# Second products of the FFNs: the residual is loaded into the sum tiles before the first product, and every product is added to it

## The chip, the cores and the metric

The kernel runs on one core of one Trainium2 chip. The metric is the device time of one execution in microseconds (us). The median of 3 runs before the change is 2866.83 us (2863.23 to 2869.62).

## What is computed

One layer of a hybrid decoder over 1024 prompt tokens and 64 sample tokens, width 1024, all in float32: a half-step SwiGLU FFN, a token mixer (a pooling branch and a state-space branch), and a second half-step FFN, each behind an RMSNorm and added to its input, then a final RMSNorm. The change touches only how the two FFNs end:

```python
def swiglu(x, w_in, w_out):
    gu = x @ w_in
    g, u = gu[..., :D_FF], gu[..., D_FF:]
    return (jax.nn.silu(g) * u) @ w_out
...
        x = x + 0.5 * swiglu(rmsnorm(x, norm_ffn1[l]), ffn1_w_in[l], ffn1_w_out[l])
...
        x = x + 0.5 * swiglu(rmsnorm(x, norm_ffn2[l]), ffn2_w_in[l], ffn2_w_out[l])
```

D_MODEL is 1024 and D_FF is 2816. The plain x of the sum is the residual.

## The kernel before

Data lies with channels on the 128 partitions and tokens along the row. The 1088 tokens are two "halves": h=0 with 512 columns, h=1 with 576 (`NTOK`). A [128 x 512] or [128 x 576] tile of x belongs to a channel block m (0 to 7) and a half. Every float32 operand of a matmul is split into a high part (`wh`, `hh`) made by ScalarE (ACT) and a low part (`wl`, `hr`/`hp`) made by VectorE (DVE), and three matmuls (high x high, high x low, low x high) stand for one.

**The second matrix of an FFN** (`second`, lines 772 to 874) is multiplied by a Strassen-like scheme of seven products, in the order `ORDER2 = "4251736"`. For product p the weights are one block of `w_out` or the sum or difference of two (`BLOCKS2`; the addition is on POOL, L760), and the other operand is one of seven combinations of the hidden activations, which lie in HBM as `xq[p]` since the FFN's first half. Each product runs over 11 pieces `kk` of the hidden width, in two blocks, m0=0 and m0=2. A block has 132 matmuls and ends with four PSUM banks. So each FFN has 14 such blocks; the two stretches are called here the first and the second stage.

**Evictions.** At the end of a block, `add` (L815) puts each bank into the sum tiles `C[m, h]`, 16 tiles of the pool "fx" (17 buffers). `INTO2` says where product p goes and with which sign. The first contribution to a place is a copy with scale 0.5 on ACT (L828); later ones are `scalar_tensor_tensor` on DVE (L830): sum = 0.5 * product + sum. By `INTO2`, product 4 is wholly first contributions (12 copies in each of its two blocks), and products 2 and 5 each have 4 first and 6 later ones in a block: 40 copies in a stage. Evictions are traced at the priority `HP_EV` = 60.

**The residual** (L800). x lies in HBM as `xspill[h][m]`. During products 5, 1, 7 and 3 (`RES2`) four of its tiles each are loaded into `xr` tiles of the pool "act" (42 buffers) by SP's DMA queue (L805) and added to the sums on DVE (L812).

**What sets the order.** The code is written in the order of the matmuls; `pe[0]` counts estimated TensorE time. A `Chain` is a generator with a due time: after each `kk` piece `tick()` steps the chains that are due, and what a step issues is traced at that place. `fetch_x` (L777) is such a chain: it loads the 11 pieces of the next product's operand (`t`, L791: `hr<-xq`, or `hp<-xq` for products 4, 5 and 7, whose first eight pieces lie in the pool "pair" with 8 buffers) and splits them on ACT (L781) and DVE (L782) some loads later. Weights come by L754 (`wraw`, 6 buffers), are split by L768 on ACT and L769 on DVE (`wh`, `wl`, 3 buffers each), at the priority `HP` = 40. The framework orders the instructions of each engine by priority and readiness when the program is built, and each engine then takes its own in that order. All DMAs named here are issued from SP. The sums of hidden activations that make the last piece of `xq` are still done on POOL (L677 to L698) while product 4 begins; its place in the code is after the second run of weights (`run[0] == 2`, L859).

`after(0, ...)` is called once product 7 is done and begins the next norm for h=0; `half` and `after(1, ...)` take h=1 after products 3 and 6.

Of the kernel before, what the change touches and what calls it, by code (L numbers as in the profile page):

```python
# [11 lines left out]
AF = mybir.ActivationFunctionType  # L12
ALU = mybir.AluOpType

P = 128
# [14 lines left out]
HALVES = (0, 1)  # L30
NTOK = (512, 576)
# [30 lines left out]
ORDER2 = "4251736"  # L62
# [3 lines left out]
INTO2 = {"1": ((0, 0, 1), (1, 1, 1)), "2": ((1, 0, 1), (1, 1, -1)), "3": ((0, 1, 1), (1, 1, 1)),  # L66
         "4": ((0, 0, 1), (1, 0, 1)), "5": ((0, 0, -1), (0, 1, 1)), "6": ((1, 1, 1),), "7": ((0, 0, 1),)}
IN_PAIRS = "457"
RES2 = {2: (0, (4, 5, 6, 7)), 3: (0, (0, 1, 2, 3)), 4: (1, (0, 1, 2, 3)), 5: (1, (4, 5, 6, 7))}
X_AT, X_PACE, X_LAG, X_LAG_END = 2.0, 1.6, 6, 4  # L70
RES_PACE = 3.0
SUM_PACE = 1.5


# [1 line left out]
def tile_hybrid_pool_ssd_macaron(  # L76
# [10 lines left out]
    V, S, T, G = nc.vector, nc.scalar, nc.tensor, nc.gpsimd  # L87
    dma = nc.sync.dma_start
# [7 lines left out]
    def nm(s):  # L96
        uid[0] += 1
        return f"{s}_{uid[0]}"

    def act(shape=(P, 576), dt=F32, name="a"):  # L100
        return sp.tile(list(shape), dt, tag="act", bufs=N_ACT, name=nm(name))

    def pair(n, name="hl"):
        t = sp.tile([P, 2, 576], F32R, tag="pair", bufs=N_PAIR, name=nm(name))
        return t[:, 0, :n], t[:, 1, :n], t
# [16 lines left out]
    def fx(dt=F32, name="x"):  # L122
        if stage["name"] == "mix":
            return act((P, 576), dt, name)
        return stage["p"].tile([P, 592], dt, tag="fx", bufs=N_FX, name=nm(name))

    def psum(tag="ps", name="ps"):
        npd = stage["npd"]
        return stage["ps"].tile([P, 512], F32, tag=tag, bufs=npd if tag == "pd" else 8 - npd, name=nm(name))
# [18 lines left out]
    def start(gen, delay=0.0):  # L148
        c = Chain(gen, delay)
        chains.append(c)  # L150
        return c
# [13 lines left out]
    def finish(c):  # L165
        while not c.done:
            c.step()

    def tick():
        while chains:  # L170
            c = min(chains, key=lambda q: q.due)
            if c.due > pe[0]:
                return
            c.step()

    def mm(out, lhsT, rhs, start=True, stop=True, free=False):
        T.matmul(out, lhsT, rhs, start=start, stop=stop, skip_group_check=free)  # L177
        pe[0] += max(out.free_size(), 64) / 2400.0 * (1 if rhs.dtype == F32R else 4)
# [85 lines left out]
    xspill = [[dp.tile([P, NTOK[h]], F32, tag=f"xs{h}_{m}", name=f"xspill{h}_{m}") for m in range(KD)] for h in HALVES]  # L264
# [506 lines left out]

    def second(wo, after, half):

        X, C, touched = {p: [] for p in ORDER2}, {}, set()
        n = 2 * NQ

        def fetch_x(p, kks, pace, lag=X_LAG):  # L777
            loaded = []

            def part_x(t, a):  # L780
                S.activation(a[:, :n], t[:, :n], AF.Identity)  # L781
                V.tensor_tensor(t[:, :n].bitcast(F32R), t[:, :n], a[:, :n].bitcast(F32), op=ALU.subtract)  # L782
                X[p].append((a, t.bitcast(F32R)))

            for kk in kks:
                if p in IN_PAIRS and kk < N_PAIR:
                    a, t, _ = pair(576, "hp")
                    t = t.bitcast(F32)
                else:
                    t, a = act((P, 576), F32, "hr"), act((P, 576), F32R, "hh")  # L790
                dma(t[:, :n], xq[p][kk])  # L791
                loaded.append((t, a))
                if len(loaded) > lag:
                    part_x(*loaded.pop(0))
                yield pace
            while loaded:
                part_x(*loaded.pop(0))
                yield pace

        def residual(h, ms):  # L800
            loaded = []
            for m in ms + (None,):
                if m is not None:
                    t = act((P, NTOK[h]), name="xr")
                    dma(t, xspill[h][m])  # L805
                    loaded.append((m, t))
                    yield RES_PACE
                    if len(loaded) < 2:
                        continue
                m_, t = loaded.pop(0)  # L810
                o = C[m_, h][:, : NTOK[h]]
                V.tensor_tensor(o, o, t, op=ALU.add)  # L812
                yield RES_PACE

        def add(pt, m, side, c, sign):  # L815
            if side:
                to = [(1, NA + NQ * c, 0, NQ)]
            else:
                to = [(0, 0, 0, NQ)] if c == 0 else [(0, NQ, 0, NQ - NA), (1, 0, NQ - NA, NA)]
            new = (m, side) not in touched  # L820
            if c:
                touched.add((m, side))
            for h, at, of, w in to:
                if (m, h) not in C:
                    C[m, h] = fx(name="x")
                o = C[m, h][:, at : at + w]
                if new:
                    S.activation(o, pt[:, of : of + w], AF.Copy, scale=0.5 * sign)  # L828
                    continue
                V.scalar_tensor_tensor(o, pt[:, of : of + w], 0.5 * sign, o, op0=ALU.mult, op1=ALU.add)  # L830

        finish(start(fetch_x(ORDER2[0], range(NKK - 1), 0.0)))
        ahead = []
        for at, p in enumerate(ORDER2):
            if at + 1 < len(ORDER2):
                last = at + 2 == len(ORDER2)
                ahead.append(start(fetch_x(ORDER2[at + 1], range(NKK), *((1.4, X_LAG_END) if last else (X_PACE, X_LAG))),
                                   15.0 if last else X_AT if at else 6.0))
            if at in RES2:
                res = start(residual(*RES2[at]), 3.0)  # L840
            for m0 in (0, 2):
                pts = [[psum("ps" if j and m0 and at < 5 else "pd", "po") for _ in range(2)] for j in range(2)]
                kps = [(kp,) for kp in range(0, NKK, 2)]
                if at >= 5:
                    kps = [kps[0] + kps[1]] + kps[2:-2] + [kps[-2] + kps[-1]]
                for run in kps:
                    W2 = [(kp, min(2, NKK - kp), second_weights(wo, p, kp, min(2, NKK - kp), m0)) for kp in run]
                    for j in range(2):
                        for kp, n2, W in W2:
                            for k in range(n2):  # L850
                                while len(X[p]) <= kp + k:
                                    ahead[at - 1].step()
                                xh, xl = X[p][kp + k]
                                for i, (w, x) in enumerate(((0, xh), (0, xl), (1, xh))):
                                    for c in range(2):
                                        mm(pts[j][c][:, :NQ], W[w][:, k, j * P : (j + 1) * P], x[:, c * NQ : (c + 1) * NQ],
                                           start=kp + k == 0 and i == 0, stop=kp + k == NKK - 1 and i == 2)
                                tick()
                    if at == 0 and m0 == 0 and run[0] == 2:  # L859
                        while summing:  # L860
                            finish(summing.pop())
                        finish(start(fetch_x(p, range(NKK - 1, NKK), 0.0)))
                with tc.high_priority(HP_EV):
                    for j in range(2):
                        for c in range(2):
                            for y, side, sign in INTO2[p]:
                                add(pts[j][c], 4 * y + m0 + j, side, c, sign)
            if at in RES2:
                finish(res)
            if p == "7":  # L870
                after(0, [C[m, 0] for m in range(KD)])
            if p == "3" and half:
                half(1, [C[m, 1] for m in range(KD)])
        after(1, [C[m, 1] for m in range(KD)])
# [967 lines left out]
    for h in HALVES:  # L1842
# [9 lines left out]
        if h == 1:  # L1852
            o = []
            prep2.append((start(norm_parts(reload(0), 0, i_g2, o, 2.0)), o))
            c = prep2[0][0]
# [135 lines left out]
```

## Time and profile before

| | us |
|---|---|
| median of 3 runs | 2866.83 |
| lowest, highest run | 2863.23, 2869.62 |
| profiled execution, its time | 2863.49 |
| span of the profiled execution (first to last instruction) | 2861.7 |
| TensorE matmuls busy | 2766.0 (97% of the span) |
| VectorE busy | 1867.4 (65%) |
| ScalarE busy | 1362.0 (48%) |
| GpSimd busy | 1367.7 (48%) |
| first stage, first to last block of L856's matmuls | 528.8 to 779.1 |
| second stage | 2598.4 to 2846.2 |

The span lies 1.8 us below the profiled execution's own time. Matmul rows are pipelined and overlap, so a busy TensorE is read from its waits and from the length of a block. In the views "PE" is TensorE, "po" a block's PSUM bank, and an idle time is put down to what ended it ("<-").

### The profile page before, as it was taken

To read this page: it belongs to the slowest core of one execution; us is meant where nothing else is said; L and a number is where in the kernel's file an instruction comes from. 1 tells how busy PE (TensorE), PEld (TensorE's weight loads), DVE (VectorE), ACT (ScalarE), POOL (GpSimd) and SP (SyncE) were. 2 spreads that over 40 slices of the span, in tenths; PEclk is the share of its full clock that TensorE was granted. 3 is DMA by queue.
4 is the path that set the end of the run, shared out by engine and by line. 5 is a ranking of instruction groups with operands and counts; after the bars stand their busy time and mean duration, and the time that the engine had idled before them with its cause. 6 is when DMAs were issued, how large, how long until landed. Compare 5 with 4: busy or idle time off the path is not lost.

```text
span 2861.7 us, 54691 instructions
## 1 busy us (share of the span) xinstructions
PE 2766.0 (97%) x19834; PEld 2595.6 (91%) x19834; DVE 1867.4 (65%) x2904; ACT 1362.0 (48%) x3024; POOL 1367.7 (48%) x1406
## 2 busy tenths in 40 slices
PE   7999999999999999999999999999999999999998
PEld 5999999899889999999997887678999999998997
DVE  6665655777884485867675767766665544457775
ACT  5444444643454555554545545566233434435433
POOL 6566576443442365554632334233225766664432
PEclk9999999999999999999999999999999999999999
DMA  4565554798745455554368679887775323337965
GB/s 134 174 212 189 180 166 143 245 299 254 242 130 162 146 174 166 183 159 138 96 218 251 203 247 283 259 270 226 232 252 172 115 95 95 99 111 258 292 207 183
DMA packets 533488, 548.02 MB, mean 192 GB/s; under 512 B 42836, under 2 KB 373704, under 8 KB 533208
## 3 DMA queue, kind: packets, MB, share of 16 engines
q1 hardware_dynamic: 533200, 544.51, 59.8%
q8 instruction: 156, 2.56, 0.4%
q14 instruction: 116, 0.95, 0.1%
q10 hardware_dynamic: 16, 0.00, 0.0%
HBM read 391.82 MB, written 152.78 MB: 190 GB/s over the span
## 4 chain that ended last, share of the span: by engine, by line
PE 74%; DMA 9%; DVE 6%; issue 4%; POOL 3%; ACT 3%; SPq 1%; POOLq 0%; ACTq 0%; DVEq 0%
PE pw L177 45%; PE po L177 8%; PE pso L177 4%; PE pg L177 3%; PE pbp L177 3%; PE pwo L177 3%; PE pu L177 2%; DMA hr<-xq 2%; DMA hp<-xq 1%; DMA ea<-eacd 1%; DMA wraw<-in_ffn_w_out_dram 1%; PE pgm L177 1%; DMA ab<-acsd 1%; DVE hr L782 1%; PE pyd L177 1%
## 5 line engine op out<-in xcount | busy, mean ns | idle before, releaser
L177 PE MATMUL pw<-X,wh 128*128 128x288 f32 (+2 forms) x2832 | 626.1, 310 | 4.1 <-ACT t L605 2.7
L177 PEld LDWEIGHTS pw<-X,wh 128*128 128x128 f32 x2832 | 461.4, 189 | 26.0 <-ACT t L605 3.2
L177 PE MATMUL pw<-X,wl 128*128 128x288 f32 (+1 forms) x1644 | 473.0, 288 | 0.4 <-DVE wl L460 0.4
L460 DVE TENSOR_TENSOR wl<-s,wh 128x512 fp32r<-128x512 f32 x288 | 243.0, 846 | 246.0 <-ACT wh L459 234.5
L177 PE MATMUL pw<-hl,wh 128*128 128x256 f32 (+1 forms) x1536 | 391.8, 328 | 3.6 <-ACT t L581 2.2
L453 POOL TENSOR_TENSOR s<-wraw,wraw 128x512 f32<-128x512 f32 x144 | 197.9, 1374 | 330.2 <-DVE wl L460 198.9
L177 PE MATMUL pw<-hi,wh 128*128 128x288 f32 x1120 | 331.7, 296 | 2.1 <-DVE t L617 1.4
L177 PE MATMUL pw<-hi,wl 128*128 128x288 f32 x1120 | 329.8, 294 | 0.0
L177 PE MATMUL pw<-lo,wh 128*128 128x288 f32 x1120 | 329.7, 294 | 0.0
L177 PEld LDWEIGHTS pw<-X,wl 128*128 128x128 f32 x1644 | 311.1, 189 | 0.6 <-DVE wl L460 0.6
L177 PE MATMUL pw<-hl,wl 128*128 128x256 f32 x1072 | 300.7, 280 | 1.2 <-DVE wl L460 1.2
L177 PEld LDWEIGHTS pw<-hl,wh 128*128 128x128 f32 x1536 | 258.8, 189 | 25.0 <-ACT t L581 2.9
L760 POOL TENSOR_TENSOR ws<-wraw,wraw 128x512 f32<-128x512 f32 x120 | 172.0, 1440 | 204.4 <-DVE wl L769 74.7
L460 DVE TENSOR_TENSOR wl<-wraw,wh 128x512 fp32r<-128x512 f32 x216 | 178.3, 825 | 125.3 <-ACT wh L459 120.5
L459 ACT ACTIVATE wh<-s 128x512 fp32r<-128x512 f32 x288 | 181.0, 629 | 136.2 <-PE pw L177 111.8
L177 PEld LDWEIGHTS pw<-hi,wh 128*128 128x128 f32 x1120 | 210.5, 188 | 9.0 <-DVE t L617 2.0
L177 PEld LDWEIGHTS pw<-lo,wh 128*128 128x128 f32 x1120 | 210.6, 188 | 0.0
L177 PEld LDWEIGHTS pw<-hi,wl 128*128 128x128 f32 x1120 | 210.1, 188 | 0.0
L459 ACT ACTIVATE wh<-wraw 128x512 fp32r<-128x512 f32 x216 | 135.6, 628 | 152.1 <-PE pw L177 129.2
L177 PEld LDWEIGHTS pw<-hl,wl 128*128 128x128 f32 x1072 | 203.0, 189 | 2.2 <-DVE wl L460 2.2
L177 PE MATMUL po<-hh,wh 128*128 128x272 f32 x848 | 177.9, 291 | 8.1 <-ACT wh L768 7.2
L177 PE MATMUL pso<-yhl,wh 128*128 128x288 f32 (+1 forms) x768 | 179.2, 338 | 2.1 <-DVE yhl L375 1.7
(403 smaller groups left out, 6743.3 us busy)
## 6 DMA issues: line engine op xcount, KB each, us to landing
wraw<-in_ffn_w_out_dram SPq DMA_DIRECT2D x240, 256.0 KB
wraw<-in_ffn_w_in_dram SPq DMA_DIRECT2D x188, 256.0 KB
wraw<-in_w_in_dram SPq DMA_DIRECT2D x144, 256.0 KB
wh<-part SPq DMA_DIRECT2D x116, 256.0 KB
wl<-part SPq DMA_DIRECT2D x116, 256.0 KB
hr<-xq SPq DMA_DIRECT2D x106, 272.0 KB
xq<-s SPq DMA_DIRECT2D x66, 272.0 KB
xq<-g SPq DMA_DIRECT2D x62, 272.0 KB
```

What stands on the lines that cost most here:

```text
L177: T.matmul(out, lhsT, rhs, start=start, stop=stop, skip_group_check=free)
L453: G.tensor_tensor(t, a, b, op=op)
L459: S.activation(wh, a, AF.Copy)
L460: V.tensor_tensor(wl, a, wh.bitcast(F32), op=ALU.subtract)
L760: G.tensor_tensor(s, raws[0], raws[1], op=ALU.subtract if p in MINUS2 else ALU.add)
L782: V.tensor_tensor(t[:, :n].bitcast(F32R), t[:, :n], a[:, :n].bitcast(F32), op=ALU.subtract)
```

## The change

The residual chain and its table go. A new generator `sums_of` loads the residual straight into the sum tiles. It is started in each of the two blocks of product 4, after the second run of weights, with a delay of 2.0 and one load per 1.0 us of estimated TensorE time, eight tiles for that block; what is not yet loaded at the block's end is issued there, ahead of the evictions. All contributions are then DVE additions.

```diff
-RES2 = {2: (0, (4, 5, 6, 7)), 3: (0, (0, 1, 2, 3)), 4: (1, (0, 1, 2, 3)), 5: (1, (4, 5, 6, 7))}
...
-RES_PACE = 3.0
+RES_PACE = 1.0
...
-        def residual(h, ms):
...
-                    t = act((P, NTOK[h]), name="xr")
-                    dma(t, xspill[h][m])
...
-                V.tensor_tensor(o, o, t, op=ALU.add)
...
+        def sums_of(ms):
+            for m in ms:
+                for h in HALVES:
+                    C[m, h] = fx(name="x")
+                    dma(C[m, h][:, : NTOK[h]], xspill[h][m])
                     yield RES_PACE
...
-            new = (m, side) not in touched
-            if c:
-                touched.add((m, side))
             for h, at, of, w in to:
-                if (m, h) not in C:
-                    C[m, h] = fx(name="x")
                 o = C[m, h][:, at : at + w]
-                if new:
-                    S.activation(o, pt[:, of : of + w], AF.Copy, scale=0.5 * sign)
-                    continue
                 V.scalar_tensor_tensor(o, pt[:, of : of + w], 0.5 * sign, o, op0=ALU.mult, op1=ALU.add)
...
-            if at in RES2:
-                res = start(residual(*RES2[at]), 3.0)
...
+                    if at == 0 and run[0] == 2:
+                        load_c = start(sums_of((m0, 4 + m0, m0 + 1, 5 + m0)), 2.0)
+                if at == 0:
+                    while not all((4 * y + m0 + j, h) in C for y in range(2) for j in range(2) for h in HALVES):
+                        load_c.step()
...
-            if at in RES2:
-                finish(res)
```

More of the change, by code (lines that the diff above doesn't have):

```diff
@@ L772, in second @@
     def second(wo, after, half):
-        X, C, touched = {p: [] for p in ORDER2}, {}, set()
+        X, C = {p: [] for p in ORDER2}, {}
         n = 2 * NQ
@@ L798, in fetch_x @@
                 yield pace
-        def residual(h, ms):
-            loaded = []
-            for m in ms + (None,):
-                if m is not None:
-                    t = act((P, NTOK[h]), name="xr")
-                    dma(t, xspill[h][m])
-                    loaded.append((m, t))
-                    yield RES_PACE
-                    if len(loaded) < 2:
-                        continue
[L810 to L813, printed above, removed]
+        def sums_of(ms):
[3 more added lines that the diff above has]
+                    dma(C[m, h][:, : NTOK[h]], xspill[h][m])
+                    yield RES_PACE
         def add(pt, m, side, c, sign):
@@ L819, in add @@
                 to = [(0, 0, 0, NQ)] if c == 0 else [(0, NQ, 0, NQ - NA), (1, 0, NQ - NA, NA)]
-            new = (m, side) not in touched
-            if c:
-                touched.add((m, side))
             for h, at, of, w in to:
-                if (m, h) not in C:
-                    C[m, h] = fx(name="x")
                 o = C[m, h][:, at : at + w]
-                if new:
-                    S.activation(o, pt[:, of : of + w], AF.Copy, scale=0.5 * sign)
-                    continue
                 V.scalar_tensor_tensor(o, pt[:, of : of + w], 0.5 * sign, o, op0=ALU.mult, op1=ALU.add)
```

## The prediction

> **What bounds the kernel now.** The page comes first: TensorE is busy nearly throughout, so a change elsewhere counts only by how long TensorE waits.
>
> ```profile
> span 2861.7 us, 54691 instructions
> PE 2766.0 (97%) x19834; PEld 2595.6 (91%) x19834; DVE 1867.4 (65%) x2904; ACT 1362.0 (48%) x3024; POOL 1367.7 (48%) x1406
> ```
>
> The span plus 1.8 us is the profiled execution's time, 2863.49 us, which lies 3.3 us below the median of the runs, 2866.83. I make the sum against the former and add it to the latter. Next, busy time by window, here with product 4's two blocks (528.8 and 546.9), product 2's, and stretches of products 5 and 1, then product 4's second block in the second stage:
>
> ```profile
> core 0: us, PE busy (x) PEld busy (x) DVE busy (x) ACT busy (x) POOL busy (x), PEclk, DMA share, GB/s
> 528.80:546.90 18.10, 17.14 (x134) 16.70 (x133) 8.80 (x11) 3.75 (x8) 10.41 (x10) 1.00 0.65 216
> 546.90:564.80 17.90, 16.86 (x135) 16.64 (x133) 14.58 (x18) 13.15 (x31) 4.75 (x3) 1.00 1.08 362
> 564.80:581.90 17.10, 17.03 (x132) 16.81 (x133) 11.09 (x16) 9.69 (x26) 9.74 (x7) 1.00 0.87 274
> 581.90:598.60 16.70, 16.70 (x134) 16.70 (x133) 10.03 (x18) 6.36 (x13) 7.73 (x7) 1.00 1.00 327
> 635.10:668.90 33.80, 33.72 (x264) 33.51 (x265) 32.48 (x49) 16.73 (x32) 17.51 (x12) 1.00 0.92 300
> 2615.80:2634.10 18.30, 16.81 (x134) 16.60 (x132) 14.10 (x18) 13.37 (x31) 4.90 (x3) 1.00 1.07 361
> ```
>
> A block without a wait takes 16.70 us (581.90), at the full granted clock. Product 4's second block has the DMA engines full (share 1.08, 362 GB/s), and DVE and ACT fuller than any other block near it. The first has room in all three. How much there is to win or lose stands in TensorE's waits, by stretch: product 4 and its end (528 to 567), then products 2 to 3, then product 6; and the second stage in two stretches (2598 to 2640, 2640 to 2847):
>
> ```profile
> PE po L177 <- ACT wh L768: 1.0, 1, 1.0
> PE po L177 <- ACT hh L781: 0.7, 1, 0.7
> PE po L177 <- DVE hr L782: 0.2, 1, 0.2
> ```
> ```profile
> PE po L177 <- ACT wh L768: 2.7, 2, 1.6
> PE po L177 <- DVE wl L769: 1.1, 2, 0.6
> ```
> ```profile
> PE po L177 <- DVE wl L769: 2.4, 3, 1.1
> PE po L177 <- DVE hr L782: 2.3, 1, 2.3
> ```
> ```profile
> PE po L177 <- ACT wh L768: 1.5, 1, 1.5
> PE po L177 <- DVE wl L769: 1.5, 1, 1.5
> ...
> ```
> ```profile
> PE po L177 <- ACT wh L768: 2.0, 2, 1.2
> PE po L177 <- DVE wl L769: 0.6, 1, 0.6
> ```
>
> So all that products 2 to 6 could give back is 2.7+1.1+2.4+2.3 = 8.5 us in the first stage and 2.6 in the second, 11.1 us in all. There is no such ceiling on a loss. The chain of waits tells what ends the wait at product 2's start (564.8):
>
> ```profile
> 539.83 0.39 SPq L791
> ...
> 544.28 5.87 DMA hr<-xq
> 550.22 5.96 DMA hr<-xq
> 556.27 7.18 DMA hp<-xq
> 563.53 0.67 ACT hp L781
> 564.86 0.69 DVE wl L769
> 565.60 4.43 PE po L177 x33
> ```
>
> At 539.83 SP issues the last operand piece of product 4. From 544 to 563.5 the path is a queue of transfers, one behind the other: the next is issued as an earlier one lands, and each takes 6 to 7 us because the engines are full. Product 2's first weights stand behind them, since ACT takes `hp` (product 5's operand) before `wh`.
>
> **Part by part.** The instructions that go or change are these, over both stages:
>
> ```profile
> L828 ACT ACTIVATE x<-po x80: 203/396/471, 548.6 to 2710.2; 128x272 f32<-128x272 f32 x48, 128x240 f32<-128x240 f32 x16, 128x32 f32<-128x32 f32 x16
> L830 DVE SCALAR_TENSOR_TENSOR x<-po,x x160: 171/423/443, 581.7 to 2846.4; 128x272 f32<-128x272 f32 x96, 128x240 f32<-128x240 f32 x32, 128x32 f32<-128x32 f32 x32
> L812 DVE TENSOR_TENSOR x<-x,xr x32: 673/747/1852, 589.0 to 2797.5; 128x512 f32<-128x512 f32 x16, 128x576 f32<-128x576 f32 x16
> L805 SPq DMA_DIRECT2D xr<-xspill x32: 326/406/1331, 584.2 to 2790.8; - x32
>   DMA xr<-xspill: 20.5, 9
> ```
>
> *ACT.* 80 copies of 0.396 us go, 31.7 us of ACT time. None was on the path: no TensorE wait above is on L828. Gain 0. What is late next is still `hp` and `wh`, which wait for transfers.
>
> *DVE, evictions.* 80 additions of 0.423 us (the mixture of shapes is the same as in L830's row) come: 33.8 us, 24 of them a stage in product 4 (12 after each block, 5.1 us) and 4 after each block of products 2 and 5 (1.7 us). After product 4's first block they fall into the window that has 14.58 us of DVE work in 17.90: 14.58 + 5.1 = 19.7, which is 1.8 us more than fits. Below is 0, because low-priority operand splits (`hr`, needed only from 564.8 at one per 1.5 us) can be put later; above is 1.8 us a stage if the first `wl` of product 2 goes with them. I take 0.5 a stage, near the lower end, because weight splits have the higher priority in the code.
>
> A rule of the Trainium skill speaks against this part: "TensorEngine Tiling (Array Packing)", section "PSUM Bottleneck", advises to use both ScalarE and VectorE to empty PSUM. By it the 1.8 us would be paid in full, and the sum below would be 2.6 us higher over the two stages; the trace has ACT at 13.15 of 17.90 us in that window, so there both are in use today.
>
> *DVE, residual.* 32 additions go, 0.747 us each, 23.9 us, and with them the 20.5 us in which DVE stood still for `xr` (the last row above: 9 waits). This is 22 us of DVE time a stage, spread over products 5, 1, 7 and 3. DVE has 32.48 us of work in 33.80 us in product 1, so it does matter there. Of the waits above I strike: the 1.1 us on `wl` in products 2 to 3 and 1.1 of the 2.7 on `wh`, 1.0 of the 4.7 in product 6 (only norm work and operand splits are left there, and no residual is in that window), and in the second stage the 0.6 on `wl` and the 1.2 on `wh`, whose chain holds a residual load itself:
>
> ```profile
> 2686.21 4.29 DMA xr<-xspill
> 2690.57 5.68 DMA hp<-xq
> 2696.33 7.10 DMA hp<-xq
> ```
>
> Together 1.1+1.1+1.0+0.6+1.2 = 5.0 us. Bounds: 0, and the whole 11.1.
>
> *The loads.* 16 loads a stage move from products 5 to 3 into product 4, on the same queue of SP. They bring 8 x 128 x 512 x 4 B and 8 x 128 x 576 x 4 B = 4.46 MB; at the 362 GB/s of the full window that is 12.3 us of the DMA engines, and 16 x 0.406 = 6.5 us of SP. Their place in the code is behind the last piece of product 4's operand, which is the chain's start, and ahead of product 5's `hp`: the first eight among product 2's `hr` loads, the others behind these. Queued behind them on SP are `hr`, `wraw` and `hp`; TensorE waits for these through ACT and DVE. So they enter exactly the queue that the path follows. How much of 12.3 us reaches TensorE depends on the slack of product 2's weights. POOL's sums of weight pairs and their splits show it:
>
> ```profile
> 554.84 1.63 POOL L760 TENSOR_TENSOR ws<-wraw,wraw 128x512 f32<-128x512 f32 x1 [15.45 <-DVE hr L782]
> ...
> 565.12 1.56 POOL L760 TENSOR_TENSOR ws<-wraw,wraw 128x512 f32<-128x512 f32 x1 [2.65 <-DMA wraw<-in_ffn_w_out_dram]
> ```
> ```profile
> 564.10 0.61 ACT L768 ACTIVATE wh<-ws 128x512 fp32r<-128x512 f32 x1
> 564.86 0.68 DVE L769 TENSOR_TENSOR wl<-ws,wh 128x512 fp32r<-128x512 f32 x1
> ```
>
> The first pair is summed at 556.5 and, with 0.61 + 0.68 us, could be split by 557.8; TensorE wants it at 564.8: slack 7.0. The fourth is summed at 566.7, could be split by 568.0, and is wanted three runs later, 564.8 + 3 x 16.70/5.5 = 573.9 (11 pieces are 5.5 runs of two): slack 5.9. A delay of 12.3 us leaves 5.3 to 6.4 us of new wait. Bounds: 0 if the loads land in time unused today, 12.3 if `wh` stays behind `hp` on ACT. I take 6.0 a stage, nearest to the weights' own rows.
>
> *Tail.* The last product and what follows keep their instructions; 0.
>
> Sum: 2 x (6.0 + 0.5) - 5.0 = +8.0 us: 2871.5 for the profiled execution, 2875 for the median. The end runs over the bounds: 0 - 11.1 to 2 x (12.3 + 1.8) = +28.
>
> **The rivals.** *Faster (the loads hide).* The first block of product 4 moves 216 GB/s where 362 are possible: (362 - 216) x 18.1 us = 2.6 MB, more than the first eight loads (2.2 MB). Were they issued there, and the other eight behind the weights, the queue would pay little, and of the 11.1 us of waits some 7 could go: 2860. It decides by whether product 2's first `wl` is ready by 564.8. Against it: half of that block is over at 539.83, and the loads stand in the code behind the operand piece that SP issues only then. The Trainium skill supports it ("DMA: Bandwidth & Descriptors", section "Anatomy of one DMA — SWDGE (gpsimd) path"): 2.0 us plus bytes at 436 GB/s, by which one such load would be an estimated 2.6 us, and land long before its eviction; the trace, on another path, has 5.87 to 7.18 us for like sizes. Chance 0.23.
>
> *No change that can be told (same).* The queue's delay is about 2.5 us a stage and cancels the 5.0: 2867. For it speaks that ACT and DVE order `wh` and `wl` by readiness and could take them before `hp`. Chance 0.15.
>
> *Much slower (the evictions hold DVE up).* An eviction now waits for its tile's load, on an engine that takes its work in order; `wl` and `hr` are queued behind it, and TensorE behind those. That this happens shows in the residual's 20.5 us of DVE waits in 9 cases, 2.3 each. Eight loads of 0.26 to 0.29 MB need 6.1 us at 362 GB/s; if half of this, 3 us, is waited at the first tiles after each of product 4's two blocks and a further 1 us at a later tile, that is 8 us a stage on top: 8 + 16 = +24, 2891. It decides when the loads land later than a block's end by more than the weights' slack of 6 to 7 us. Chance 0.14.
>
> **How the numbers follow.** The forecast, +8, has 0.48; its own range, +2 to +16, is 2869 to 2883. A measurement of this kernel can tell about 0.2%, 5.7 us, from no change. Of the forecast 0.40 lies above that and 0.08 within; the much slower case adds 0.14: slower 0.54. The same case gives 0.15 and the fringe of the faster one 0.05: same 0.28. Faster keeps 0.18. The range reaches from just below the faster case to just above the much slower one, 2859 to 2893, and leaves out their outer parts, some 0.15.
>
> **What would show it.** Right: 80 more rows on L830's successor and none on ACT for `x<-po`; DMA share about 1.0 through both blocks of product 4 and into product 2; at the boundary 4 to 2 a TensorE wait that grows from 1.0 and 3.0 us to 6 or more; fewer waits on `wl` in products 5 to 3. Wrong: the blocks of product 2 begin as early after product 4's start as now (36.0 us, from 528.8 to 564.8), or DVE waits for `x<-xspill` longer than some 4 us at a time, which is the third rival.

## The result, and the profile after

The kernel with the change takes 2879.61 us (median of 6 runs, 2877.26 to 2884.62); the kernel before took 2868.22 us beside it (6 runs, 2863.23 to 2875.22). The ratio is 1.0043, with a 95% interval of 1.0029 to 1.0056: slower by 0.43%, about 12 us. The forecast was 2875 us within 2859 to 2893, so sign and size came close; not every term of its sum did.

The profiled execution of the kernel after is the slowest of its six, and that of before (2863.49 us) is close to the fastest of its six. The two spans differ by 20.8 us, the medians by 11.4 us. So a difference between the two traces is read below for its place, and its price is taken from the medians and from the experiments.

The page of the kernel after, its span and its engines:

```profile
span 2882.5 us, 54600 instructions
PE 2775.8 (96%) x19834; PEld 2607.2 (90%) x19834; DVE 1882.1 (65%) x2952; ACT 1344.7 (47%) x2944; POOL 1364.5 (47%) x1406
```

ACT lost 80 instructions, and DVE has 48 more: 80 additions less 32 of the residual. The work itself is what the diff says. The loss is in waits, so the next view is busy time by window, product 4's two blocks first, then product 2's first block, then products 5 to 6 (608.3 to 789.6) and, last, product 4's second block in the second stage and products 5 to 6 there:

```profile
core 0: us, PE busy (x) PEld busy (x) DVE busy (x) ACT busy (x) POOL busy (x), PEclk, DMA share, GB/s
531.60:550.60 19.00, 17.47 (x134) 17.03 (x133) 9.38 (x13) 3.72 (x8) 10.42 (x10) 0.98 0.64 216
550.60:573.30 22.70, 18.50 (x134) 17.89 (x132) 14.67 (x38) 8.53 (x16) 1.26 (x1) 0.94 1.06 374
573.30:591.60 18.30, 18.29 (x132) 18.30 (x133) 17.19 (x17) 9.18 (x16) 9.75 (x7) 0.91 1.01 332
...
608.30:789.60 181.30, 173.70 (x1335) 171.79 (x1334) 142.82 (x221) 74.18 (x131) 77.06 (x61) 0.98 0.77 247
...
2629.50:2653.50 24.00, 18.52 (x134) 18.08 (x132) 14.62 (x37) 8.81 (x16) 1.27 (x1) 0.93 1.06 370
...
2687.90:2867.00 179.10, 173.71 (x1376) 172.82 (x1376) 123.95 (x206) 69.46 (x132) 65.53 (x47) 1.00 0.64 209
```

The same view of the kernel before, products 5 to 6 of each stage:

```profile
598.60:779.10 180.50, 171.75 (x1335) 168.95 (x1334) 143.07 (x221) 76.50 (x141) 78.31 (x59) 1.00 0.82 261
...
2669.30:2846.20 176.90, 174.25 (x1376) 172.92 (x1375) 125.63 (x206) 71.36 (x142) 64.01 (x45) 1.00 0.69 225
```

Product 4's second block, which took 17.9 and 18.3 us, takes 22.7 and 24.0. The DMA engines are full in it (share 1.06), as they were before. Products 5 to 6, from which the residual went, take 0.8 and 2.2 us more, not less. DVE's work in product 4's second block is the same (14.67 us against 14.58): the additions took the room of operand splits that were put later, so that product 2's first block now has 17.19 us of DVE work where it had 11.09.

What TensorE waits for, in four stretches: product 4 and its end (531 to 575) and the rest of the first stage (575 to 790), then the same two of the second stage (2611 to 2658, 2658 to 2868):

```profile
PE po L176 <- ACT wh L767: 4.2, 2, 3.2
PE po L176 <- ACT hh L780: 1.3, 1, 1.3
PE po L176 <- DVE hr L781: 0.2, 1, 0.2
```
```profile
PE po L176 <- DVE wl L768: 4.5, 4, 2.6
...
```
```profile
PE po L176 <- ACT wh L767: 5.5, 2, 3.5
PE po L176 <- DVE wl L768: 0.7, 1, 0.7
...
```
```profile
PE po L176 <- DVE wl L768: 5.3, 4, 1.9
...
```

At product 4 the wait on `wh` grew from 1.0 to 4.2 us in the first stage. On `wl`, behind product 4, it did not shrink: 4.5 and 5.3 us, where before it was 3.5 and 0.6. So the relief that the forecast struck off is missing.

Why `wh` is late shows in the order in which SP issues its DMAs. First the kernel before, then the kernel after (start, duration, line, how many in a row):

```profile
540.30 1.43 SPq L754 DMA_DIRECT2D wraw<-in_ffn_w_out_dram  x3
541.78 5.25 SPq L791 DMA_DIRECT2D hr<-xq  x9
548.03 1.82 SPq L754 DMA_DIRECT2D wraw<-in_ffn_w_out_dram  x3
```
```profile
543.10 2.97 SPq L803 DMA_DIRECT2D x<-xspill  x3
546.11 1.38 SPq L790 DMA_DIRECT2D hr<-xq  x3
...
555.44 0.38 SPq L753 DMA_DIRECT2D wraw<-in_ffn_w_out_dram  x1
...
564.27 1.17 SPq L753 DMA_DIRECT2D wraw<-in_ffn_w_out_dram  x2
```

Before, three of the coming weights go out at 540.30, ahead of the operand pieces. After, the residual's loads and operand pieces alternate, and the first of those weights goes out at 555.44: 23.8 us after product 4's start (531.6) and not 11.5 (528.8). These three are the last weights of product 4's own second block. Product 2's first pair goes out behind them, at 564.27 and not at 548.03: 32.6 us after product 4's start and not 19.2. The chain of waits of the kernel after joins the queue there:

```profile
547.05 4.68 DMA hr<-xq
...
551.75 5.81 DMA hr<-xq
...
557.58 5.06 DMA x<-xspill
...
565.06 6.11 DMA wraw<-in_ffn_w_out_dram
...
571.33 1.27 POOL ws L759
```

A residual load stands between an operand piece and a weight, and POOL sums product 2's first weight pair at 571.33 to 572.6, where before it had it at 556.5. The slack of 7.0 us is gone, and TensorE begins product 2 at 573.3, 41.7 us after product 4's start and not 35.9. Not all of the wait on `wh` stands there. Of the 4.2 us, 1.0 falls inside product 4's second block, on the block's own late weights, and of the 5.5 us of the second stage 3.5 do, at 2642.17:

```profile
2635.58 5.81 DMA wraw<-in_ffn_w_out_dram
...
2641.49 0.64 ACT wh L767
...
2642.17 3.05 PE po L176 x12
```

The clock column holds something that the forecast had not counted. Three stretches of 3.4 us at the end of product 4's first block, of the kernel after:

```profile
546.40:549.80 3.40, 1.87 (x13) 1.43 (x12) 1.63 (x3) 1.70 (x3) 0.00 (x0) 1.00 0.91 313
549.90:553.30 3.40, 3.40 (x17) 3.40 (x16) 1.81 (x7) 2.05 (x4) 0.00 (x0) 0.50 1.04 381
553.30:556.70 3.40, 3.40 (x29) 3.40 (x28) 1.57 (x5) 0.58 (x1) 0.00 (x0) 1.00 1.03 388
```

In the first, TensorE stands still for 1.5 us. In the second, the granted clock is 0.50, and 17 matmuls run where the third has 29. The 12 that are missing cost 12 x 3.4/29 = 1.4 us. The trace after has five such stretches within the two stages (549.9, 573.8, 648.9, 768.3 and 2642.2), and the trace before has none.

### The profile page after: what moved, and what is told of

Read it like the earlier page. It is cut to its first block, busy times and chain, and to the rows that moved or that the text cites. A ratio compares the mean times of both kernels' runs of the same rounds, so it can differ in the third digit from the quotient of the medians.

```text
span 2882.5 us, 54600 instructions
## 1 busy us (share of the span) xinstructions
PE 2775.8 (96%) x19834; PEld 2607.2 (90%) x19834; DVE 1882.1 (65%) x2952; ACT 1344.7 (47%) x2944; POOL 1364.5 (47%) x1406
## 4 chain that ended last, share of the span: by engine, by line
PE 73%; DMA 9%; DVE 6%; POOL 4%; issue 4%; ACT 2%; SPq 1%; POOLq 0%; ACTq 0%; DVEq 0%
PE pw L176 45%; PE po L176 6%; PE pso L176 5%; DMA wraw<-in_ffn_w_out_dram 4%; PE pg L176 3%; PE pbp L176 3%; PE pwo L176 3%; PE pu L176 2%; POOL ws L759 1%; DMA ea<-eacd 1%; PE pgm L176 1%; DVE hr L781 1%; PE pyd L176 1%; POOL s L676 1%; PE pst L176 1%
## 5 line engine op out<-in xcount | busy, mean ns | idle before, releaser
L176 PE MATMUL po<-hh,wl 128*128 128x272 f32 x848 | 177.6, 292 | 6.6 <-DVE wl L768 6.6
```

## The experiments

Ratios are to the kernel before, run beside it on the same chip, with their 95% intervals. "Product 4" is the time from its first matmul to product 2's first, in the first and the second stage of the profiled execution. "Clock" is the granted clock, the mean over a kernel's runs; that of the kernel before has 77 runs behind it, beside the experiments. There its medians were 2866.96, 2867.05 and 2867.24 us (experiments 1, 2, 5 and 7; 3, 6, 8 and 9; 4, 10 and 11), and the ratios are to these.

| kernel | median, us | ratio | product 4, us | clock |
|---|---|---|---|---|
| before | 2868.22 | 1 | 35.9, 35.7 | .9932 |
| after | 2879.61 | 1.0043 [1.0029, 1.0056] | 41.7, 42.0 | .9917 |
| 1 copies on DVE | 2869.18 | 1.0006 [0.9996, 1.0016] | 34.8, 35.8 | .9932 |
| 2 extra loads | 2876.39 | 1.0031 [1.0021, 1.0042] | 41.8, 42.3 | .9906 |
| 3 tiny extra loads | 2863.21 | 0.9985 [0.9977, 0.9994] | 35.1, 35.5 | .9930 |
| 4 half the extra loads | 2868.66 | 1.0012 [1.0003, 1.0021] | 34.9, 35.9 | .9918 |
| 5 no residual | 2864.35 | 0.9988 [0.9979, 0.9997] | 35.1, 36.0 | .9930 |
| 6 no residual, copies on DVE | 2867.75 | 1.0008 [0.9999, 1.0017] | 35.1, 37.6 | .9930 |
| 7 loads early | 2883.06 | 1.0052 [1.0039, 1.0066] | 46.0, 46.1 | .9900 |
| 8 loads on ACT's queue | 2883.29 | 1.0062 [1.0049, 1.0074] | 44.0, 43.5 | .9904 |
| 9 loads split | 2865.14 | 0.9997 [0.9988, 1.0006] | 35.9, 36.6 | .9930 |
| 10 operand later | 2870.40 | 1.0014 [1.0006, 1.0023] | 34.8, 35.8 | .9926 |
| 11 loads split, operand later | 2864.59 | 0.9991 [0.9981, 1.0000] | 35.9, 36.6 | .9931 |

Two theories stood against each other. By the queue theory, the forecast's, the 16 loads in product 4 hold up the weights behind them. By the DVE theory, the evictions that came to DVE hold up `wl`.

**1. The evictions alone.** The kernel before, with its 80 copies on DVE:

```diff
-                    S.activation(o, pt[:, of : of + w], AF.Copy, scale=0.5 * sign)
+                    V.tensor_scalar_mul(o, pt[:, of : of + w], 0.5 * sign)
```

> The kernel before, with only the first contributions moved: the 80 copies of a product into its sum tile are made by DVE instead of ACT; the residual is loaded and added late, as before. Queue theory (the 16 residual loads in product 4 hold up the weights behind them on SP's queue): the time stays within 3 us of before, and TensorE's waits in product 4 and at its end stay near the 5.1 us of before (1.9 and 3.2 in the two stages). DVE theory (the additions that came to DVE hold up the weight splits wl in its in-order queue): 5 us or more slower, with new waits on wl of 1 to 3 us at the start of products 5, 1 and 7.

It took 1.0006 of the time before, and the interval holds 1. Product 4 is as long as before. The DVE theory falls as the cause of the loss. By the page of the Trainium skill that the prediction named against this part ("TensorEngine Tiling (Array Packing)", section "PSUM Bottleneck"), both ScalarE and VectorE should be used to empty PSUM; giving up ScalarE for these copies shows no cost of its own here that can be measured.

**2. The loads alone.** The kernel before, with 16 loads a stage in the place where the change has them, into tiles that nobody reads:

```diff
+        def unused(ms):
+            for m in ms:
+                for h in HALVES:
+                    dma(act((P, NTOK[h]), name="xe"), xspill[h][m])
+                    yield 1.0
...
+                    if at == 0 and run[0] == 2:
+                        extra = start(unused((m0, 4 + m0, m0 + 1, 5 + m0)), 2.0)
+                if at == 0:
+                    finish(extra)
```

> The kernel before, with 16 more loads of the residual in each stage at the places where the change has them, into tiles that nothing reads; evictions, late residual loads and additions are those of before. Queue theory: TensorE's waits in product 4 and at its end rise from 5.1 us to about 12 us over the two stages, as after the change, and the time rises by 7 to 16 us. DVE theory: within 3 us of before.

1.0031, some 9 us, without a single changed eviction. What TensorE waits for around product 4, in this kernel's two stages:

```profile
PE po L177 <- ACT wh L768: 6.9, 1, 6.9
...
```
```profile
PE po L177 <- ACT wh L768: 7.5, 1, 7.5
...
```

The wait stands on the very line that the forecast named, and is 6.9 and 7.5 us where it was 1.0 and 1.5. The loads make this wait by themselves, as the queue theory has it.

**3. The same instructions with few bytes.** As experiment 2, but each load brings 16 columns, 8 KB:

```diff
-                    dma(act((P, NTOK[h]), name="xe"), xspill[h][m])
+                    dma(act((P, NTOK[h]), name="xe")[:, :16], xspill[h][m][:, :16])
```

> The kernel before with the 16 extra loads a stage of the earlier run (which cost 0.31%), at the same places, but each of 16 columns, 8 KB in place of 256 to 288 KB. If the price is that of the bytes on the DMA engines: within 2 us of before, TensorE's waits at product 4's end near before's. If it is that of SP, which issues 16 more and waits for earlier ones before it does (0.4 us each, 6.5 us a stage): 5 to 9 us slower, as with whole loads.

The loss is gone, so it is the bytes and not the 16 issues on SP. The kernel is even 0.15% faster than the kernel before, although it only adds work. That was not expected. In the first stage of its profile TensorE's wait on `wh` around product 4 is gone, and the longest left is the one below (in the second stage 0.7 us on `wh` are left); that adding instructions changed the order in which others are placed is the likely reason, but no run isolates it.

```profile
PE po L177 <- ACT hh L781: 1.0, 1, 1.0
...
```

**4. Half of the bytes.** As experiment 2, with the tiles of h=0 only, 2.1 MB a stage and one per 2.0 us:

```diff
-                for h in HALVES:
-                    dma(act((P, NTOK[h]), name="xe"), xspill[h][m])
-                    yield 1.0
+                dma(act((P, NTOK[0]), name="xe"), xspill[0][m])
+                yield 2.0
```

> The kernel before with 8 extra loads a stage in product 4 (the h=0 tiles, 256 KB each, 2.1 MB) where the earlier run had 16 (4.46 MB, 0.31%). If the price is in proportion to the bytes: 0.15%, 4 to 5 us slower than before. If the weights' slack of 6 to 7 us must be used up first, as the prediction's step has it (2.1 MB are 5.8 us at 362 GB/s): within 2 us of before.

1.0012: somewhat over a third of experiment 2's price, 3.4 us (0.9 to 6.0), between the two expectations. In the profile product 4 is no longer than before, so the price here is not a wait at its end; there the 2.1 MB stay within the slack. The trace has two stretches at half clock in the first stage (624.6 and 761.2), and the clock over the runs is lower (.9918); that these are the price was not tried by itself.

**5. What the residual costs at all.** The kernel before with `RES2 = {}`, which leaves the residual of both FFNs out:

```diff
-RES2 = {2: (0, (4, 5, 6, 7)), 3: (0, (0, 1, 2, 3)), 4: (1, (0, 1, 2, 3)), 5: (1, (4, 5, 6, 7))}
+RES2 = {}
```

> The kernel before with the residual of both FFNs left out (neither loaded nor added), so that 32 loads and 32 DVE additions and their 20.5 us of DVE waits are gone and nothing comes in their place. It prices what the change could win at most. If the relief of DVE and of the queue in products 5 to 3 is worth the 5.0 us that the prediction struck off, 4 to 6 us faster than before; if it is worth nothing, within 2 us; at the very most 11 us, all of TensorE's waits there.

0.9988, 3.4 us (0.9 to 6.0): that is what a residual without any cost would win in this order of the instructions. Its 20.5 us of DVE waits and 23.9 us of DVE work were nearly all beside TensorE's path. After product 4's start in the first stage (530 to 779) this kernel still waits 4.7 us on `wl`:

```profile
PE po L177 <- DVE wl L769: 4.7, 4, 1.7
...
```

With 0.5 us in the second stage these are 5.2 us, where the kernel before has 5.6. So `wl` comes late without the residual too; what was charged to the residual was mostly not its doing.

**6. The change without its loads.** Experiment 1's edit and `RES2 = {}` together, again without the residual:

```diff
-                    S.activation(o, pt[:, of : of + w], AF.Copy, scale=0.5 * sign)
+                    V.tensor_scalar_mul(o, pt[:, of : of + w], 0.5 * sign)
...
+RES2 = {}
```

> The first contributions as copies on DVE and the residual of both FFNs left out (neither loaded nor added): the change without its loads. Queue theory: 2863 to 2869, that is within 3 us of the kernel with the residual left out and copies on ACT (2864), and 9 us or more below after; then the loads alone make up the difference. DVE theory: 2872 or more.

1.0008: the evictions on DVE together with the relief come out at +2.3 us (-0.3 to +4.9), and not at the gain that the forecast had. From experiment 5 to this one, the same copies cost 0.20%, where by experiment 1 they cost 0.06%; the two intervals overlap. One place can be named: TensorE waits 2.6 us for `wl` at product 1's start in the first stage, and ahead of that `wl` stand the ten evictions of product 5's last block, all on DVE now. The kernel after has the same wait (2.6 us at 648.7), with the same ten ahead of it.

**7. The loads earlier.** The kernel after, with the first eight loads issued ahead of product 4's blocks and the second eight where the first were:

```diff
+            if at == 0:
+                finish(start(sums_of((0, 4, 1, 5))))
...
-                    if at == 0 and run[0] == 2:
-                        load_c = start(sums_of((m0, 4 + m0, m0 + 1, 5 + m0)), 2.0)
+                    if at == 0 and m0 == 0 and run[0] == 2:
+                        load_c = start(sums_of((2, 6, 3, 7)), 2.0)
```

> The kernel after, with each set of eight loads issued one step earlier: the first eight before product 4's first weights are multiplied, ahead of the sums on POOL for which SP waits, the second eight at the place of the first. The first eight then use transfers' time that lies idle today. Queue theory: half or more of the 7.5 us that product 4's waits have grown by goes, so 4 to 9 us faster than after (2871 to 2876). DVE theory: as after, 2877 to 2882.

This missed: 1.0052, no better than the change. SP's DMAs in this kernel:

```profile
519.97 5.56 SPq L803 DMA_DIRECT2D x<-xspill  x8
525.92 0.38 SPq L753 DMA_DIRECT2D wraw<-in_ffn_w_out_dram  x1
...
539.92 0.32 SPq L702 DMA_DIRECT2D xq<-g  x1
...
543.62 0.43 SPq L753 DMA_DIRECT2D wraw<-in_ffn_w_out_dram  x1
```

The loads now stand ahead of product 4's own weights. One weight gets out behind them; then SP takes the stores of `xq` in order, up to 539.92, and they wait for sums that POOL is still making. The next weight goes out at 543.62. The wait moved from product 4's end into its first block, 7.5 us at 550.25:

```profile
PE po L176 <- ACT wh L767: 7.5, 1, 7.5
...
```

So the faster rival, whose first eight loads use the spare 2.6 MB of product 4's first block, has no way in by this place: in front of the stores SP has weights to bring, and behind them the block is half over.

**8. Another queue.** The kernel after, with the loads on ACT's DMA queue:

```diff
-                    dma(C[m, h][:, : NTOK[h]], xspill[h][m])
+                    nc.scalar.dma_start(C[m, h][:, : NTOK[h]], xspill[h][m])
```

> The kernel after, with its 32 loads issued from ACT's DMA queue instead of SP's. If what counts is that the loads stand ahead of the weights in one queue in order, most of the loss goes: 2868 to 2873. If it is the DMA engines' time, which both queues share, the loss stays within half: 2874 to 2884. ACT's own issue time, about 0.4 us each and 6.5 us a stage, may cost 1 to 3 us on top, as ACT is nearly full in product 4.

1.0062. The loads now start earlier, and the transfers share the same engines: the first window here moves more than before (285 GB/s), the second is full, 26 us long, and TensorE's wait of 8.6 us on `wh` ends near its close.

```profile
528.00:546.00 18.00, 16.51 (x129) 16.08 (x128) 7.75 (x9) 2.65 (x5) 10.15 (x10) 1.00 0.87 285
546.00:572.00 26.00, 17.41 (x137) 17.20 (x136) 16.01 (x31) 11.72 (x20) 3.99 (x4) 0.91 1.04 352
```

That agrees with the Trainium skill ("DMA: Bandwidth & Descriptors", section "Issuing engines are not separate DMA queues"), by which DMAs started by different engines run on the same DMA engines. SP is no longer held up at the old place: it issues three weights at 539.17, 11.5 us after product 4's start, as before the change. So being behind the loads in SP's order is not what the price needs; the transfers' time is enough. ACT's own work may have been disturbed too: three issues at 556.43 span 3.33 us, in which it does nothing else. That part is not told apart here.

**9. Fewer bytes at the tight place.** The kernel after, where product 4 loads the h=0 tiles and only the first 32 columns of h=1, which it needs; the other 544 columns, which are first written in products 2 and 5, come during these:

```diff
-                    dma(C[m, h][:, : NTOK[h]], xspill[h][m])
+                    n_ = NA if h else NTOK[0]
+                    dma(C[m, h][:, :n_], xspill[h][m][:, :n_])
...
+        def side_of(ms):
+            for m in ms:
+                dma(C[m, 1][:, NA : NTOK[1]], xspill[1][m][:, NA:])
+                yield 3.0
...
+            if at in (1, 2):
+                load_s = start(side_of((4, 5, 6, 7) if at == 1 else (0, 1, 2, 3)), 2.0)
...
+                if at in (1, 2):
+                    finish(load_s)
```

> The kernel after, with half of the residual's bytes taken out of product 4: there only what product 4 itself adds to is loaded (8 tiles of h=0 and 8 pieces of 32 columns of h=1); the other 544 columns of the h=1 tiles are loaded during products 2 and 5, ahead of their first additions. Queue theory, by bytes: half of the loss goes, 2870 to 2875. If the number of loads ahead of the weights counts and not their size: as after, 2877 to 2882 (16 loads still stand there). DVE theory: as after.

0.9997: the median has the whole loss gone, with every eviction of the change still on DVE. Product 4 is back at 35.9 and 36.6 us. Its wait on `wh` in the first stage, and the windows of product 4's second and product 2's first block:

```profile
PE po L176 <- ACT wh L767: 0.6, 1, 0.6
...
```
```profile
547.30:565.10 17.80, 17.22 (x134) 16.75 (x133) 12.26 (x28) 8.03 (x15) 1.46 (x1) 1.00 1.03 341
565.10:586.40 21.30, 18.52 (x135) 18.31 (x134) 17.62 (x28) 9.10 (x16) 10.41 (x7) 0.92 1.06 360
```

The DMA engines stay full, and product 2 pays: it takes 39.1 and 38.8 us, where the kernel before took 33.9 and 35.2. In the first stage the chain of waits runs over a residual load that lands at 564.8, then eleven additions of product 4's second block, then product 2's `wl` behind them, for which TensorE waits 2.8 us, until 569.07:

```profile
560.38 4.40 DMA x<-xspill
...
564.86 2.77 DVE x L819 x11
567.62 1.40 DVE wl L768
...
569.07 5.94 PE po L176 x33
```

So the DVE theory's mechanism exists, at this place. What makes up for it comes later. Products 5, 1 and 7 together, of this kernel and then of the kernel before, in both stages:

```profile
604.20:704.40 100.20, 100.20 (x794) 100.20 (x793) 80.88 (x129) 41.78 (x73) 46.78 (x34) 1.00 0.85 272
...
2679.80:2780.20 100.40, 100.40 (x793) 100.20 (x793) 81.26 (x128) 40.66 (x70) 45.57 (x35) 1.00 0.81 262
```
```profile
598.60:703.10 104.50, 102.05 (x794) 100.56 (x793) 80.03 (x127) 44.39 (x84) 46.02 (x33) 1.00 0.85 273
...
2669.30:2772.80 103.50, 101.65 (x795) 100.56 (x794) 79.11 (x124) 42.57 (x81) 46.12 (x32) 1.00 0.81 263
```

In this kernel's profiled execution, the slowest of its eleven, TensorE waits for nothing in them; the kernel after took 105.8 and 105.6 us. By these traces products 4 and 2 are still 9.6 us longer than before over both stages, and products 5 to 6 are 7.5 us shorter. The split takes back 2.8 us of the change's delay in products 4 and 2, and most of the rest is relief behind them. Why the relief is here and not in experiment 6 (108.1 and 104.2 us for the same three products) is open; it is not the residual alone, since experiment 2's kernel, which keeps it, has 102.1 us twice.

**10. Is the wait at product 4's end worth winning?** The kernel before, with the operand chains starting later (`X_AT` from 2.0 to 7.0), so that `wh` comes ahead of `hp`:

```diff
-X_AT, X_PACE, X_LAG, X_LAG_END = 2.0, 1.6, 6, 4
+X_AT, X_PACE, X_LAG, X_LAG_END = 7.0, 1.6, 6, 4
```

> The kernel before with the loads of the next product's operand started 7.0 in place of 2.0 us of estimated TensorE time into each product (all but the first and last), so that product 5's operand (hp) stands behind product 2's first weights on SP, ACT and DVE. If it is hp ahead of wh that makes the waits at product 4's end (1.0 and 3.0 us): these go below 1 us each and the time falls by 2 to 4 us. If they come from the transfers being full: within 2 us of before, with the waits where they were or at a later product.

1.0014. TensorE's waits around product 4 sum to 1.2 and 2.5 us in the two stages (1.9 and 3.2 before), and those behind it in the second stage to 4.6 us (2.6 before). The theory that the place of `hp` ahead of `wh` is what there is to win falls; why the kernel became slower, by 4 us (1.7 to 6.6), is not settled.

**11. The two together.** The edits of experiments 9 and 10 on the kernel after (`side_of`, and `X_AT` at 7.0):

> The split loads (which measured 0.9997 of before) with the same later start of the operand loads. If the order of hp and wh is what is left of the loss at product 4's end and in product 2 (2.8 and 2.4 us there): 2860 to 2864, below both kernels. If not: within 2 us of the split loads, 2863 to 2867.

2864.59 us, 0.9991 [0.9981, 1.0000]. It lies clearly below the kernel after, and at the edge of what can be told from the kernel before. From experiment 9 it differs by 0.6 us, so the later start adds nothing that can be measured. Products 5, 1 and 7 run without a wait here too (100.2 and 100.6 us). Of the versions that compute the whole result, only experiment 3's, the kernel before with loads that nobody reads, has an interval wholly below 1, and why is not known.

## Why the prediction was right, and where it was not

**The main term, the loads: right.** The forecast had 2 x 6.0 = 12.0 us. The loads by themselves cost 0.31% in experiment 2, 8.9 us (6.0 to 12.0), and the change with its loads less the change without them is 0.43% - 0.08% = 0.35%, some 10 us (an estimated 5 to 15, from the two intervals). In the traces product 4 and what follows it up to product 2 grew by 41.7 + 42.0 - 35.9 - 35.7 = 12.1 us. The mechanism is the one given: bytes, since 8 KB loads cost nothing; weights that come late; a wait on `wh`. Its parts differ from the working, though. The forecast worked from the slack of product 2's weights; product 4's own last weights stood behind the loads as well, and 1.0 us in the first stage and 3.5 in the second are waits for these. TensorE's waits up to product 2's first matmul sum to 5.7 and 6.2 us where they were 1.9 and 1.7, so they bring 8.3 of the 12.1 us. Two of the stretches at half clock lie in product 4 and bring 2.8; 1.0 us is not accounted for. That 12.0 fits the traces so closely is in part luck, since neither term beside the wait on product 2's weights was in it. Over the runs the mean clock falls from .9932 to .9917; as TensorE works nearly throughout, that is an estimated 0.0015 x 2870 = 4.3 us of the 11.4, from only six runs of the kernel after.

**The evictions on DVE: small by themselves.** 1.0 us was forecast for both stages; experiment 1 has 0.06%, 1.7 us (-1.1 to +4.6). They are not free at every place: behind product 5's second block ten additions stood ahead of a `wl`, and TensorE waited 2.6 us for it at 648.7 (the longest on `wl` in the first stage's rows), as it does in experiment 6. The prediction had given the additions behind products 2 and 5 no price.

**The relief in products 5 to 3: the step that failed.** The prediction struck off 5.0 us, with bounds of 0 and 11.1, because DVE would be free of 22 us a stage. In the traces these products took 0.8 and 2.2 us more. Without any residual at all the kernel before gains 3.4 us (experiment 5), and with the evictions moved as well none is left (experiment 6, +2.3 us where the sum had -5.0 + 1.0 = -4.0). The reason that it gave, that DVE has 32.48 us of work in 33.80 in product 1, was not enough: before the change TensorE waits for no `wl` in product 1, full as DVE is. The runs measure relief and evictions together; how the miss of some 6 us divides between the two stays open, since relief of more than the forecast's size does appear behind the split loads of experiment 9. In this change the lower bound, 0, was the one to be near to. So the sum came out at 8 where the runs have 11.4.

**The rivals.** *Much slower*: its mechanism is in the trace, and small. An eviction does wait for its load, but 8 times in all and never longer than 1.9 us; the additions and these waits in the kernel after (in experiment 9 such a wait did delay product 2):

```profile
L813 DVE SCALAR_TENSOR_TENSOR x<-po,x x240: 171/423/444, 550.0 to 2867.3; 128x272 f32<-128x272 f32 x72, 128x240 f32<-128x240 f32 x30, 128x32 f32<-128x32 f32 x18
...
  DMA x<-xspill: 7.7, 8
```

*Faster*: the spare room in product 4's first block was not used (216 GB/s as before), and experiment 7 shows why one earlier place does not open it. By the page of the Trainium skill that stood behind it ("DMA: Bandwidth & Descriptors", section "Anatomy of one DMA — SWDGE (gpsimd) path"), a load would land an estimated 2.6 us after its issue; in the chain above, on another path, transfers of like size take 4.7 to 6.1 us, one behind the other. *No change*: its cancelling relief was not there.

**What was to show it.** Product 2 begins 41.7 and not 35.9 us after product 4; the waits there grew by the rows above, though to 4.2 and 5.5 us on `wh` and not to the 6 forecast. DMA's share reached 1.06 in the second block but stayed at 0.64 in the first. Fewer waits on `wl` behind product 4 was wrong.

## What to carry to other kernels

Before moving transfers to an earlier place, look whether the DMA engines have room in that window and what stands behind the place on the issuing queue: the price is the bytes that push the next weights back, less the weights' slack. Where the bytes are needed only later, split the load and let each part come where it is first written; here that took back the whole loss of the medians. Look then at the next place too: the split kernel still paid in product 2, and gained it back later. Busy time and waits of an engine beside the path give a bound for the relief, not its size; a kernel that leaves the operation out altogether measures it, for that order of the instructions.

## What the runs showed of the hardware

Waits much shorter than 3.4 us can cost more than their own length. In the trace after, stretches of 3.4 us at a granted clock of 0.50 follow waits of 1.3 to 3.5 us, each costing some 1.4 us more; one wait of 1.69 us at 750.5 and one of 1.98 us at 2653.5 passed without. The five stretches begin at whole multiples of 3.41 us from the first (7, 29, 64 and 613). In the 3.41 us just ahead of each, on this grid, TensorE stood idle for 1.5, 3.0, 2.7, 2.3 and 3.3 us. The wait of 1.98 us lies across two such windows, some 1.0 us in each; that of 1.69 lies in one, and so the border is not settled. No run tries this by itself. The Trainium skill ("TensorE: Matmul & The Clock Gate", section "What's actually happening") has a free-running window of 3413 ns and a fall to half clock after at least one idle window. The stretches' length and their grid agree; that a whole idle window is needed does not, as the window ahead of 549.9 had 1.5 us of waits. The kernels with long waits have the lower clocks over their runs too (.9900 to .9917 in four of them, .9932 before), and among the 77 runs of the kernel before a lower clock goes with a longer time (correlation -0.56), so part of the scatter of one and the same kernel lies there.
